# Accumulating transfers for three of the four sums of weights of a pair, and sums of h in steps

## The chip, the core and the metric

The kernel runs on one core of one Trainium2 chip. The metric is the time of one execution on the device in microseconds (us); for a kernel it is the median over its runs. The engines have their usual names: TensorE (PE, with its weight loads as PEld), VectorE (DVE), ScalarE (ACT), GpSimd (POOL) and SyncE (SP), which here only issues transfers.

## The reference, cut to what matters

The kernel computes one layer of a streaming encoder for one sequence of 512 tokens and width 2048, and a last RMSNorm. Everything is float32. An adaLN-modulated RMSNorm gives h, one wide projection of h gives the inputs of an mLSTM branch (4 heads of 256) and of a chunked attention branch (8 heads of 128) and two gates, and both branches come together in one output projection.

```python
h = rmsnorm(x, norm_g) * (1.0 + scale[:, None]) + shift[:, None]
proj = h @ w_in
(mq, mk, mv, mo, mz, mi, mf, aq, ak, av, az, g_m, g_a) = split_columns(proj)
y_m = mlstm_branch(mq, mk, mv, mo, mz, mi, mf, b_if, conv_w, conv_b, mh_norm_g)
y_a = chunk_attention_branch(aq, ak, av, az, rel_bias)
merged = jax.nn.sigmoid(g_m) * (y_m @ w_proj_m) + jax.nn.sigmoid(g_a) * (y_a @ w_proj_a)
return x + gate[:, None] * (merged @ w_out)        # and then rmsnorm(..., final_norm_g)
```

The change touches `h @ w_in`: how some of the columns of this projection are computed.

## The kernel before

**Products in two halves.** Float32 factors are split into a high and a low float16 part (`split`, lines 166 and 167: ScalarE writes `hi`, VectorE then writes `lo` from the source and `hi`), and TensorE makes three products out of them (hi*hi, hi*lo, lo*hi). Each group of weights gets a power of two as its scale: ScalarE squares each loaded half unit (`do_squares`, line 235), TensorE adds the sums up over the partitions (`do_tots`, through `tot_of`, line 150), and VectorE makes the scale and its inverse from the exponent (`scale_of`, lines 157 to 162).

**Units and jobs.** A unit is 128 columns (or 256 columns by half the depth) of a weight matrix, and is loaded as two transfers of 512 KB (128 partitions of 1024 float32). `jobs()` lists what is to be made, in order: single units (`u`, two chunks of 48 matmuls), tokens (`t`, two units, four chunks), projections (`p`) and pairs (`s`). A chunk is planned at 2.6 us in a pair and at 5.2 us in the others (`CHUNK_US`). A pair computes two units at once by Strassen's scheme in Winograd's form, with seven half-size products in place of eight: seven chunks of 24 matmuls. There are 32 pairs: 27 in which the two units belong to one group and share a scale (`same`), and five that pair a q with a k and have two scales (mixed).

**What a pair needs.** Its weights are four quarters: x11 and x21, the halves of the first unit, and x12 and x22, those of the second. Of them and of four sums seven weight tiles are made: 11, 22, t2, 21, t3, t1, t4, in that order (`of_pair`). The sums are made in place by VectorE: `p22` makes two of them after tile 22 is split, `p2` the third (line 273, or 275 in a mixed pair), `p21` the fourth (line 293). On the other side h is needed in its four quarters and four sums of quarters: `h_sums` makes them with four operations on 128x2048 elements (line 551) and four splits, all of them behind the first chunk of the first job. `strassen` (line 939 on) runs the seven products and adds them into the two results out of PSUM: ScalarE copies (lines 963, 964, 977), VectorE adds scaled results (line 947, and 986 for the fifth product).

**Buffers and order.** Loads go into a ring of eight buffers (`NST`); a load is issued when the oldest buffer's last reader is done (`can_load`, `free`). Weight tiles go into nine buffers (`NW`), so tiles are made up to nine ahead of their use. `stream(c)` stands behind every chunk and keeps everything going by a planned clock: loads (`do_dma`, on SP's queue), squares 7.0 us behind the load, totals 2.5 us behind the squares, scales, and then tiles (`make_after`). The order on TensorE at the beginning is written out by hand; elsewhere the framework sets the order on each engine when the kernel is built, and an engine then takes its instructions strictly in that order. The attention and the mLSTM heads run beside the jobs as generators (`side`, `advance`), and `heads` is started with the first job.

Of the kernel before, what the change touches and what calls it, by code (L numbers as in the profile page):

```python
# [9 lines left out]
F32 = mybir.dt.float32  # L10
# [33 lines left out]
def jobs():  # L44

    def s(kind, h, kind2=None):
        return ("s", (kind, h, 0), (kind2 or kind, h + (kind2 is None), 0))

    def u(kind, h, part=0):
        return ("u", (kind, h, part))

    def t(kind, h):
        return ("t", (kind, h, 0), (kind, h, 1))

    j = [u("k", 2), t("v", 0), t("v", 2), s("z", 2), s("q", 3, "k"), s("q", 4, "k"), t("v", 4), s("z", 4),
         s("q", 5, "k"), u("if", 0), s("q", 6, "k"), t("v", 6), s("z", 6), s("q", 7, "k")]
# [24 lines left out]
def block_kernel(ctx: ExitStack, tc: tile.TileContext, A, out):  # L83
# [98 lines left out]

    groups_w, group_of, loads = [], {}, []
    for j, job in enumerate(todo):
        i = first[j]
        if job[0] == "s":
            loads += [(i, 0), (i + 1, 1), (i + 1, 0), (i, 1)]
            gs = [[i, i + 1]] if job[1][0] == job[2][0] else [[i], [i + 1]]
# [26 lines left out]
    def width(x):  # L215
        return KT * 8 if x[0] == UIF else HW

    def do_dma(n=None):

        while at["dma"] < (len(loads) if n is None else n) and can_load() and not (n is None and at["other"]):  # L220
            x = loads[at["dma"]]
            st[x] = stage_tile(f"st_{x[0]}_{x[1]}")
            i, part = x
            src = A["w_if"] if i == UIF else A["w_u"][i - 1 if i > UIF else i][:, part * HW:(part + 1) * HW]
            nc.sync.dma_start(st[x]["tile"][:, 0:width(x)], src)
            when["dma", at["dma"]] = at["clock"]
            at["dma"] += 1

    def do_squares(n):
        while at["sq"] < min(n, at["dma"]):  # L230
# [3 lines left out]
            with nc.allow_low_precision(reason="only the exponent of the sum is used"):  # L234
                ACT.activation(junk(width(x)), st[x]["tile"][:, c], AF.Square, accum_out=ssq[x])  # L235
            when["sq", at["sq"]] = at["clock"]
            at["sq"] += 1

# [24 lines left out]
    def of_pair(j):  # L263
# [4 lines left out]

        def sub_or_mix(to, a, b, op, ratio):

            a, b, to = (st[x]["tile"] for x in (a, b, to))
            if same or ratio is None:
                V.tensor_tensor(to, a, b, op)  # L273
            else:
                V.scalar_tensor_tensor(to, b, ratio, a, ALU.mult, ALU.add)

        r = []

        def p22():
            tile_w("22", x22)  # L280
            if not same:
                r.append(times(scs[i][0], scs[i + 1][1], -1.0, f"r{i}"))
                r.append(times(scs[i + 1][0], scs[i][1], 1.0, f"n{i}"))
            sub_or_mix(x22, x22, x12, ALU.subtract, None)
            sub_or_mix(x12, x12, x11, ALU.subtract, r[0] if r else None)

        def p2():
            sub_or_mix(x11, x11, x22, ALU.add, r[1] if r else None)
            tile_w("t2", x11)

        def p21():
            tile_w("21", x21)
            V.tensor_tensor(st[x21]["tile"], st[x21]["tile"], st[x11]["tile"], ALU.subtract)
            st[x11]["free"] = True
# [57 lines left out]
    def stream(c):  # L352
# [5 lines left out]
        do_squares(n)  # L358
        do_tots(wait=2.5)
        do_scales()  # L360
# [185 lines left out]

    def h_sums():

        for to, a, b, op in (("22", "21", "22", ALU.add), ("21", "11", "21", ALU.subtract),
                             ("11", "22", "11", ALU.subtract), ("12", "12", "11", ALU.subtract)):  # L550
            V.tensor_tensor(of_h(to), of_h(a), of_h(b), op)
        for s, q in (("s4", "12"), ("s2", "11"), ("s3", "21"), ("s1", "22")):
            split(H[s][:, 0], H[s][:, 1], of_h(q), s_h)

# [344 lines left out]
    def finish(u, n):  # L899
# [35 lines left out]
        elif kind in ("ga", "gm"):  # L935
            ACT.activation(n, n, AF.Tanh, scale=0.5)
            th_g[kind, h] = n

    def strassen(j):

# [13 lines left out]
        def p1():  # L954
            go("a", (i, "11"), "11")
            for m, u in enumerate((u1, u2)):
                t, f = dest(u, i + m)
                n.append(t)
                if m and group_of[i] == group_of[i + 1]:
                    iw.append(iw[0])  # L960
                else:
                    iw.append(times(scs[i + m][1], i_h, f, f"u{i + m}"))
            ACT.activation(n[0][:, HT:S], ps["a"][:, 0:HT], AF.Copy, scale=iw[0])
# [144 lines left out]
    m_pool = None  # L1108
    side.append([heads(), P_])
    since = 0.0  # L1110
    for j in range(JO):
        if j == JG:
# [13 lines left out]
        for c, e in enumerate(CHUNKS[todo[j][0]](j)):  # L1126
# [170 lines left out]
```

## Time and profile before

| | before |
|---|---|
| median of three runs | 1645.82 us (1645.82, 1649.27, 1645.82) |
| the profiled execution | 1642.06 us, its span 1640.3 us |
| TensorE busy | 1515.1 us, 92% |
| VectorE busy | 1157.4 us, 71% |
| ScalarE busy | 959.6 us, 59% |
| GpSimd busy | 26.3 us, 2% |
| read from HBM, written | 204.91 MB, 4.19 MB |

The profile is of one execution; a busy share is an average over stages with different limits, so it only says where to look. Until about 157 us the scale, the shift and the first units of the projection are made from the large adaLN matrix. Then come the jobs: attention inputs to about 506 us, the mLSTM heads to about 956 us, the gates and projections to about 1460 us, and the output. A wait is put down to what released it last. Matmuls are pipelined, so a group's mean duration is longer than the distance at which its matmuls start; the distance is what counts.

### The profile page before, as it was taken

What the parts mean: (1) busy time and instruction counts of PE and PEld (TensorE: products, weight loads), DVE (VectorE), ACT (ScalarE), POOL (GpSimd) and SP (SyncE); (2) the same over time, 40 slices, a digit from 0 to 9 for tenths busy, and PEclk for the clock granted to TensorE, in tenths of its full rate; (3) what the DMA queues carried; (4) which work ended last, traced back from release to release, by engine and by line L of the source; (5) the groups of instructions that cost most, each with busy time, mean ns of one, the idle gap of its engine ahead of it and who ended that gap; (6) DMA issues with size and microseconds to landing.
All of it is one profiled execution on the core that took longest, in us unless ns stands there. A gap on an engine that the chain in (4) does not pass through costs nothing.

```text
span 1640.3 us, 29263 instructions
## 1 busy us (share of the span) xinstructions
PE 1515.1 (92%) x12087; PEld 1202.1 (73%) x12087; DVE 1157.4 (71%) x1901; ACT 959.6 (59%) x1504; POOL 26.3 (2%) x30
## 2 busy tenths in 40 slices
PE   1799699999999999999999999999999999999997
PEld 0345578787888888888888876766776776768887
DVE  7987968766676666576566597777789897664443
ACT  3225856666476385395484677655656766775522
POOL 4100000000000000000000000000000000000000
PEclk9999899999999999999999999999999999999999
DMA  9893223323141142152141233334456533373202
GB/s 388 344 393 116 82 83 98 95 94 107 55 160 54 52 141 66 52 168 65 52 155 52 78 105 126 117 103 155 129 193 203 168 119 129 117 226 108 91 2 103
DMA packets 59637, 210.99 MB, mean 129 GB/s; under 512 B 7520, under 2 KB 12272, under 8 KB 55024
## 3 DMA queue, kind: packets, MB, share of 16 engines
q1 hardware_dynamic: 59504, 209.13, 37.3%
q8 instruction: 94, 1.54, 0.4%
q14 instruction: 39, 0.32, 0.1%
HBM read 204.91 MB, written 4.19 MB: 127 GB/s over the span
## 4 chain that ended last, share of the span: by engine, by line
PE 40%; DVE 28%; ACT 14%; DMA 11%; issue 7%; SPq 0%; ACTq 0%; DVEq 0%
DMA st<-in_w_u 8%; DVE w L167 6%; PE pre L477 5%; ACT junk L235 4%; DVE st L273 4%; ACT w L166 4%; PE po L585 3%; PE po L587 3%; PE po L586 3%; DVE w_t L167 3%; PE ps L560 3%; PE ps L562 3%; PE ps L561 3%; PE ps L587 2%; PE ps L586 2%
## 5 line engine op out<-in xcount | busy, mean ns | idle before, releaser
L167 DVE SCALAR_TENSOR_TENSOR w<-st,sc_w,w 128x1024 f16<-128x1024 f32 x227 | 288.8, 1277 | 139.2 <-ACT w L166 129.2
L235 ACT ACTIVATE junk<-st 128x1024 uint8<-128x1024 f32 x259 | 272.0, 1050 | 132.0 <-DMA st<-in_w_u 125.3
L166 ACT ACTIVATE w<-st,sc_w 128x1024 f16<-128x1024 f32 x227 | 256.0, 1136 | 34.7 <-PE ps L562 16.5
L166 ACT ACTIVATE w_t<-st,sc_w 128x1024 f16<-128x1024 f32 x128 | 145.2, 1141 | 131.3 <-DVE st L273 60.1
L167 DVE SCALAR_TENSOR_TENSOR w_t<-st,sc_w,w_t 128x1024 f16<-128x1024 f32 x128 | 163.6, 1280 | 67.7 <-ACT w_t L166 66.7
L575 PE MATMUL psb<-hs,w_t 128*128 128x256 f16 x512 | 140.2, 274 | 9.1 <-DVE c L947 9.1
L561 PE MATMUL ps<-h,w 128*128 128x256 f16 x544 | 148.3, 273 | 0.3 <-DVE h L167 0.3
L560 PE MATMUL ps<-h,w 128*128 128x256 f16 x544 | 148.3, 273 | 0.0
L562 PE MATMUL ps<-h,w 128*128 128x256 f16 x544 | 148.3, 273 | 0.0
L586 PE MATMUL ps<-w,h 128*128 128x256 f16 x512 | 140.5, 275 | 6.2 <-DVE w L167 6.2
L585 PE MATMUL po<-w,m 128*128 128x256 f16 x512 | 140.1, 274 | 2.3 <-ACT m L166 2.3
L575 PE MATMUL psa<-h,w 128*128 128x256 f16 x512 | 141.2, 276 | 0.0
L576 PE MATMUL psa<-h,w 128*128 128x256 f16 x512 | 141.1, 276 | 0.0
L577 PE MATMUL psa<-h,w 128*128 128x256 f16 x512 | 141.0, 275 | 0.0
L587 PE MATMUL ps<-w,h 128*128 128x256 f16 x512 | 140.6, 275 | 0.0
L585 PE MATMUL ps<-w,h 128*128 128x256 f16 x512 | 140.4, 275 | 0.0
L577 PE MATMUL psb<-hs,w_t 128*128 128x256 f16 x512 | 140.3, 274 | 0.0
L576 PE MATMUL psb<-hs,w_t 128*128 128x256 f16 x512 | 140.2, 274 | 0.0
L586 PE MATMUL po<-w,m 128*128 128x256 f16 x512 | 139.8, 274 | 0.0
L587 PE MATMUL po<-w,m 128*128 128x256 f16 x512 | 139.6, 274 | 0.0
L576 PEld LDWEIGHTS <-w_t 128*128 128x128 f16 x1024 | 100.5, 98 | 32.4 <-issue 20.8
L477 PE MATMUL pre<-B,wpre 128*128 128x512 f32 x224 | 100.8, 606 | 12.0 <-ACT B L446 12.0
(267 smaller groups left out, 3411.9 us busy)
## 6 DMA issues: line engine op xcount, KB each, us to landing
st<-in_w_u SPq DMA_DIRECT2D x258, 512.0 KB, 4.3
ada<-in_w_ada SPq DMA_DIRECT2D x30, 1024.0 KB, 6.9
B<-in_w_adag SPq DMA_DIRECT2D x21, 512.0 KB, 5.9
wpre<-in_w_pre SPq DMA_DIRECT2D x16, 448.0 KB, 7.4
gst<-in_w_adag SPq DMA_DIRECT2D x11, 512.0 KB, 3.6
B<-in_xT SPq DMA_DIRECT2D x4, 1024.0 KB, 8.1
xo_s<-in_x SPq DMA_DIRECT2D x24, 128.0 KB, 4.8
out<-xo_s SPq DMA_DIRECT2D x12, 256.0 KB, 2.4
```

The costliest lines, as they stand in the source:

```text
L166: ACT.activation(hi, src, AF.Copy, scale=s_)
L167: V.scalar_tensor_tensor(lo, src, s_, hi, ALU.mult, ALU.subtract)
L235: ACT.activation(junk(width(x)), st[x]["tile"][:, c], AF.Square, accum_out=ssq[x])
L560: PE.matmul(ps, lhsT=hi, rhs=xhi(k), start=(n == 0), stop=False)
L561: PE.matmul(ps, lhsT=hi, rhs=xlo(k), start=False, stop=False)
L562: PE.matmul(ps, lhsT=lo, rhs=xhi(k), start=False, stop=(n == len(ks) - 1))
L575: PE.matmul(ps, lhsT=hi, rhs=x[:, 0, k, :], start=(k == 0 and not more), stop=False, **kw)
L576: PE.matmul(ps, lhsT=hi, rhs=x[:, 1, k, :], start=False, stop=False, **kw)
L577: PE.matmul(ps, lhsT=lo, rhs=x[:, 0, k, :], start=False, stop=(k == K2 - 1), **kw)
L585: PE.matmul(ps, lhsT=xq[:, 0, k % K2, ts], rhs=w[:, 0, c], start=(k == 0), stop=False)
L586: PE.matmul(ps, lhsT=xq[:, 0, k % K2, ts], rhs=w[:, 1, c], start=False, stop=False)
L587: PE.matmul(ps, lhsT=xq[:, 1, k % K2, ts], rhs=w[:, 0, c], start=False, stop=(k == KT - 1))
```

## The change

For each of the 27 pairs with one scale three of the four sums become transfers on GpSimd's queue that add into a buffer in SBUF (`add_in`). x12 gets x11 added from HBM behind its square; VectorE then makes one sum, x11 = x12 + x22; x22 gets x12's source added from HBM; and x21 gets that sum added from SBUF. Since such a transfer only adds, the scheme is turned into one with sums in place of differences: the second unit enters with its sign turned (`-f` in `strassen`, so that each unit of a pair now has its own factor), and the sums of h are changed to suit. A pair's loads come in the order x11, x12, x22, x21 instead of x11, x22, x12, x21. The mixed pairs keep four sums on VectorE.

The pair (q3, k3) is taken apart into two single units, which come right behind k2; that leaves 31 pairs, of which four are mixed. The sums of h become eight steps, of which two are made behind each chunk from the second on, and the heads start when four of them are done. Totals of squares come 5.0 us of planned time behind the squares instead of 2.5.

```diff
-    j = [u("k", 2), t("v", 0), t("v", 2), s("z", 2), s("q", 3, "k"), s("q", 4, "k"), t("v", 4), s("z", 4),
+    j = [u("k", 2), u("q", 3), u("k", 3), t("v", 0), t("v", 2), s("z", 2), s("q", 4, "k"), t("v", 4), s("z", 4),
...
-            loads += [(i, 0), (i + 1, 1), (i + 1, 0), (i, 1)]
+            loads += [(i, 0), (i + 1, 0), (i + 1, 1), (i, 1)]
+            if job[1][0] == job[2][0]:
+                gs, t1_of[i + 1, 0] = [[i, i + 1]], (i, 0)
...
+    def add_in(to, x):
+
+        nc.gpsimd.dma_start(st[to]["tile"], x, accum_op=ALU.add)
...
+            if x in t1_of:
+                add_in(x, source(t1_of[x]))
             at["sq"] += 1
...
         def p22():
             tile_w("22", x22)
+            if same:
+                V.tensor_tensor(a(), b(), c(), ALU.add)
+                add_in(x22, source(x12))
+                return
+            r.append(times(scs[i][0], scs[i + 1][1], 1.0, f"r{i}"))
+            r.append(times(scs[i + 1][0], scs[i][1], 1.0, f"n{i}"))
+            V.tensor_tensor(c(), c(), b(), ALU.add)
+            V.scalar_tensor_tensor(b(), a(), r[0], b(), ALU.mult, ALU.add)
+
+        def p2():
             if not same:
+                V.scalar_tensor_tensor(a(), c(), r[1], a(), ALU.mult, ALU.add)
             tile_w("t2", x11)
 
         def p21():
             tile_w("21", x21)
-            V.tensor_tensor(st[x21]["tile"], st[x21]["tile"], st[x11]["tile"], ALU.subtract)
+            if same:
+                add_in(x21, a())
+            else:
+                V.tensor_tensor(d(), d(), a(), ALU.add)
             st[x11]["free"] = True
...
-        do_tots(wait=2.5)
+        do_tots(wait=5.0)
...
+    s_neg = const.tile([P, 1], F32, name="s_neg")
+    V.tensor_scalar(s_neg, s_h, -1.0, None, ALU.mult)
+
+    def sums_of_h():
+
+        of = {q: of_h(q) for q in ("11", "12", "21", "22")}
+        return [lambda: V.tensor_tensor(of["22"], of["21"], of["22"], ALU.subtract),
+                lambda: V.tensor_tensor(of["21"], of["11"], of["21"], ALU.subtract),
+                lambda: V.tensor_tensor(of["11"], of["22"], of["11"], ALU.subtract),
+                lambda: V.scalar_tensor_tensor(of["12"], of["12"], -1.0, of["11"], ALU.mult, ALU.subtract),
+                lambda: split(H["s4"][:, 0], H["s4"][:, 1], of["12"], s_h),
+                lambda: split(H["s2"][:, 0], H["s2"][:, 1], of["11"], s_h),
+                lambda: split(H["s3"][:, 0], H["s3"][:, 1], of["21"], s_h),
+                lambda: split(H["s1"][:, 0], H["s1"][:, 1], of["22"], s_neg)]
...
-                if m and group_of[i] == group_of[i + 1]:
-                    iw.append(iw[0])
-                else:
-                    iw.append(times(scs[i + m][1], i_h, f, f"u{i + m}"))
+                iw.append(times(scs[i + m][1], i_h, -f if m else f, f"u{i + m}"))
...
             if j == 0 and c == 0:
-                h_sums()
                 for i in range(1, NPRE):
                     pre_out(i)
+            elif steps:
+                for f in steps[:2]:
+                    f()
+                steps = steps[2:]
+                if len(steps) == 4:
+                    side.append([heads(), P_])
```

## Rows read from the trace of the kernel before

**Rows 1.** The page's first part: busy us, share of the span, instructions.

```profile
PE 1515.1 (92%) x12087; PEld 1202.1 (73%) x12087; DVE 1157.4 (71%) x1901; ACT 959.6 (59%) x1504; POOL 26.3 (2%) x30
```

**Rows 2.** Busy time by stretch; columns PE, PEld, DVE, ACT, POOL, clock, DMA share, GB/s.

```profile
156.00:193.00 37.00, 22.84 (x164) 17.22 (x163) 36.26 (x38) 30.81 (x38) 0.00 (x0) 0.82 0.14 45
...
956.00:1460.00 504.00, 480.89 (x3630) 350.85 (x3628) 396.27 (x584) 332.32 (x482) 0.00 (x0) 0.99 0.45 148
```

**Rows 3.** Waits of PE, 156 to 200 us: total us, times, longest us.

```profile
PE tot_w L150 <- ACT junk L235: 7.3, 4, 2.8
PE ps L586 <- DVE w L167: 6.2, 2, 3.9
```

**Rows 4.** Waits of PE, 200 us to the end.

```profile
PE psb L575 <- DVE c L947: 16.9, 20, 3.5
PE tot_w L150 <- ACT junk L235: 12.9, 14, 2.2
```

**Rows 5.** Timeline of PE, 171 to 190 us: start us, duration us, instruction.

```profile
173.38 0.27 PE L586 MATMUL ps<-w,h 128*128 128x256 f16 x1 [2.27 <-DVE w L167]
173.49 0.27 PE L587 MATMUL ps<-w,h 128*128 128x256 f16 x1
...
188.41 0.42 PE L585 MATMUL ps<-w,h 128*128 128x256 f16 x1
188.62 0.42 PE L586 MATMUL ps<-w,h 128*128 128x256 f16 x1
```

**Rows 6.** Timeline of DVE, 167 to 190 us.

```profile
167.04 2.28 DVE L551 TENSOR_TENSOR B<-B 128x2048 f32<-128x2048 f32 x1
...
179.91 6.87 DVE L167 SCALAR_TENSOR_TENSOR hs<-B,sc_h,hs 128x2048 f16<-128x2048 f32 x3
186.70 3.67 DVE L167 SCALAR_TENSOR_TENSOR w<-st,sc_w,w 128x1024 f16<-128x1024 f32 x3
```

**Rows 7.** Timeline of DVE in the gate stage, 1062 to 1084 us.

```profile
1067.18 1.22 DVE L273 TENSOR_TENSOR st<-st,st 128x1024 f32<-128x1024 f32 x1
1068.31 0.47 DVE L947 SCALAR_TENSOR_TENSOR c<-psb,tm_u,c 128x256 f32<-128x256 f32 x1
...
1069.95 1.23 DVE L273 TENSOR_TENSOR st<-st,st 128x1024 f32<-128x1024 f32 x1
```

**Rows 8.** Groups by form on DVE: count, busy us, mean ns, idle before.

```profile
L167 DVE SCALAR_TENSOR_TENSOR w_t<-st,sc_w,w_t 128x1024 f16<-128x1024 f32 x128 | 163.6, 1280 | 67.7 <-ACT w_t L166 66.7
L273 DVE TENSOR_TENSOR st<-st,st 128x1024 f32<-128x1024 f32 x86 | 104.9, 1220 | 0.9
L293 DVE TENSOR_TENSOR st<-st,st 128x1024 f32<-128x1024 f32 x32 | 39.0, 1219 | 0.3
...
L142 DVE TENSOR_SCALAR tm_u<-inv_w,inv_h 128x1 f32<-128x1 f32 x71 | 14.0, 210 | 1.3
```

**Rows 9.** Busy time of one stretch behind a wait, columns as in Rows 2.

```profile
1070.00:1075.00 5.00, 5.00 (x34) 3.89 (x33) 3.20 (x7) 3.94 (x5) 0.00 (x0) 0.68 0.01 4
```

**Rows 10.** Loads into the ring (tile st), 956 to 1460 us.

```profile
DMA to landing us min/median/max: 3.4/4.6/6.3
```

**Rows 11.** DMA issues: count, KB each, median us to landing.

```profile
st<-in_w_u SPq DMA_DIRECT2D x258, 512.0 KB, 4.3
ada<-in_w_ada SPq DMA_DIRECT2D x30, 1024.0 KB, 6.9
```

**Rows 12.** Timeline of ACT in the gate stage, 1062 to 1084 us.

```profile
1074.19 1.14 ACT L166 ACTIVATE w_t<-st,sc_w 128x1024 f16<-128x1024 f32 x1
...
1078.61 1.15 ACT L166 ACTIVATE w_t<-st,sc_w 128x1024 f16<-128x1024 f32 x1 [1.52 <-PE psb L577]
```

**Rows 13.** Waits of SP's queue: total us, times, longest us.

```profile
SPq L225 <- DVE st L293: 303.9, 29, 23.7
```

**Rows 14.** Line 468, divided over DVE and POOL: duration ns min/median/max, first and last start.

```profile
L468 DVE TENSOR_TENSOR B<-B,rstd x2: 1744/1748/1751, 28.2 to 29.9; 128x512 f32<-128x512 f32 x2
```

**Rows 15.** Line 420, a sum of the same size: duration ns min/median/max.

```profile
L420 DVE TENSOR_TENSOR gac<-gac,B x4: 685/689/692, 1155.6 to 1335.1; 128x512 f32<-128x512 f32 x4
```

More of the change, by code (lines that the diff above doesn't have):

```diff
@@ L180, in block_kernel @@
     UIF = units.index(("if", 0, 0))
-    groups_w, group_of, loads = [], {}, []
+    groups_w, group_of, loads, t1_of = [], {}, [], {}
     for j, job in enumerate(todo):
@@ L186, in block_kernel @@
         if job[0] == "s":
-            loads += [(i, 0), (i + 1, 1), (i + 1, 0), (i, 1)]
-            gs = [[i, i + 1]] if job[1][0] == job[2][0] else [[i], [i + 1]]
+            loads += [(i, 0), (i + 1, 0), (i + 1, 1), (i, 1)]
+            if job[1][0] == job[2][0]:
+                gs, t1_of[i + 1, 0] = [[i, i + 1]], (i, 0)
+            else:
+                gs = [[i], [i + 1]]
         else:
@@ L216, in width, with source @@
         return KT * 8 if x[0] == UIF else HW
+    def source(x):
+        i, part = x
+        return A["w_if"] if i == UIF else A["w_u"][i - 1 if i > UIF else i][:, part * HW:(part + 1) * HW]
+    def add_in(to, x):
+        nc.gpsimd.dma_start(st[to]["tile"], x, accum_op=ALU.add)
     def do_dma(n=None):
@@ L222, in do_dma @@
             st[x] = stage_tile(f"st_{x[0]}_{x[1]}")
-            i, part = x
-            src = A["w_if"] if i == UIF else A["w_u"][i - 1 if i > UIF else i][:, part * HW:(part + 1) * HW]
-            nc.sync.dma_start(st[x]["tile"][:, 0:width(x)], src)
+            nc.sync.dma_start(st[x]["tile"][:, 0:width(x)], source(x))
             when["dma", at["dma"]] = at["clock"]
@@ L267, in of_pair @@
         same = group_of[i] == group_of[i + 1]
[L269 to L273, printed above, removed]
-            else:
-                V.scalar_tensor_tensor(to, b, ratio, a, ALU.mult, ALU.add)
+        a, b, c, d = ((lambda x=x: st[x]["tile"]) for x in (x11, x12, x22, x21))
         r = []
@@ L280, in p22 @@
             tile_w("22", x22)
-            if not same:
[L282 to L288, printed above, removed]
+            if same:
[7 more added lines that the diff above has]
+        def p2():
+            if not same:
+                V.scalar_tensor_tensor(a(), c(), r[1], a(), ALU.mult, ALU.add)
             tile_w("t2", x11)
@@ L292, in p21 @@
             tile_w("21", x21)
-            V.tensor_tensor(st[x21]["tile"], st[x21]["tile"], st[x11]["tile"], ALU.subtract)
+            if same:
+                add_in(x21, a())
+            else:
+                V.tensor_tensor(d(), d(), a(), ALU.add)
             st[x11]["free"] = True
@@ L545, in block_kernel @@
             split(H[q][:, 0, c, :], H[q][:, 1, c, :], of_h(q)[:, c, :], s_h)
[L547 to L553, printed above, removed]
+    s_neg = const.tile([P, 1], F32, name="s_neg")
[10 more added lines that the diff above has]
+                lambda: split(H["s1"][:, 0], H["s1"][:, 1], of["22"], s_neg)]
     def feat_mm(ps, wk, xhi, xlo, ks):
@@ L958, in p1 @@
                 n.append(t)
-                if m and group_of[i] == group_of[i + 1]:
-                    iw.append(iw[0])
-                else:
-                    iw.append(times(scs[i + m][1], i_h, f, f"u{i + m}"))
+                iw.append(times(scs[i + m][1], i_h, -f if m else f, f"u{i + m}"))
             ACT.activation(n[0][:, HT:S], ps["a"][:, 0:HT], AF.Copy, scale=iw[0])
@@ L1108, in block_kernel @@
     m_pool = None
-    side.append([heads(), P_])
     since = 0.0
+    steps = sums_of_h()
     for j in range(JO):
```

## The prediction

> **What bounds the kernel now.** I read the page's first part before anything else: TensorE is busy for 92% of the span and VectorE for 71% [rows 1]. So an edit that takes work from VectorE is worth only what TensorE waits for VectorE, and the second view is therefore the busy time by stages. Between 156 and 193 us TensorE is busy for 22.84 of 37 us, at a mean granted clock of 0.82; in the gate stage (956 to 1460 us) it is busy for 480.89 of 504 us while VectorE has 396 us of work [rows 2]. The loss is dense at the start and thin afterwards. Third, TensorE's waits. From 156 to 200 us it waits 7.3 us for squares of weights on ScalarE and 6.2 us for weight tiles that VectorE splits [rows 3]. After 200 us its two largest waits are 16.9 us for VectorE's evacuations of PSUM (20 times) and 12.9 us for squares (14 times) [rows 4]; no wait for a split weight tile is among them. Fourth, the timelines. In the first stretch VectorE works through the sums of h and their splits, from 167.04 to 186.78 us, and only then splits the three weight tiles that TensorE resumes with at 188.03 us [rows 5, 6]. In the gate stage the second sum of a pair stands right behind an evacuation on VectorE, and three sums and that evacuation fill 1067.18 to 1071.18 us [rows 7].
>
> **The start.** The sums of h are four operations of 2.28 us and four splits of 2.34 us, some 18.5 us of VectorE in one block. The change deals them out two at a time from the second chunk on, and puts two single units (q3, k3) ahead of the first tokens unit. A unit is 96 matmuls that start 0.11 us apart [rows 5], about 10.4 us; so units k2, q3 and k3 keep TensorE busy for 31 us, and they need two weight tiles each, which can be split directly behind the first evacuations. The first pair, which needs the sums, is two tokens units later still. What hides the moved 18.5 us is these 31 us of single units, in which VectorE has only four tiles of q3 and k3 (5 us) and the four of v0 (5 us): 28.5 us of work. That nearly fills the cover, so I keep 3 us of new waiting for v0's tiles, with ends 0 and 6. Removed are the waits of 7.3 + 6.2 = 13.5 us [rows 3], and the slow clock behind them: at 188.41 us matmuls start 0.21 us apart instead of 0.11 [rows 5], the lower of the two levels (1.2 GHz), for at most the 5 us to the end of that stretch, so at most 2.5 us lost; I take 2.3. Added: q3 and k3 cost 192 matmuls instead of a pair's seven products of 24, so 24 more at 0.11 = 2.6 us. Sum: -13.5 - 2.3 + 2.6 + 3 = **-10.2 us** (ends -13 and -7). The attention's first step starts two chunks (10 us) later; its waits later on are for other things, so I price that at nothing, and at 2 us if the cover of its 300 us is gone.
>
> **The sums of weights.** VectorE makes 86 sums at one place and 32 at another, 1.22 us each [rows 8]; 86 = 3 x 27 + 5, so 27 pairs have one scale and five are mixed. Of the four sums of each of the 27 three go: 81 x 1.22 = 98.8 us. Each such pair now needs its own factor for the second unit: 27 x 0.21 = 5.7 us back [rows 8]. VectorE's net relief is 93 us, beside other work: TensorE's waits show only 16.9 us of it. Half of these waits I expect to go, since weight splits and other evacuations stay in the queue: **-8.5 us** (ends 0 and -16.9). One such wait, at 1065 us, is followed by 5 us at a mean clock of 0.68 [rows 9], 1.6 us lost; with that one gone, **-1.6 us**. The totals of the squares are sent to TensorE 5 instead of 2.5 us of planned time behind the squares. In single units and tokens a chunk is planned at 5.2 us, so both come to the next chunk there; only in pairs (2.6 us) does it move. Of 12.9 us I take a quarter: **-3 us** (ends 0 and -8).
>
> **The transfers.** 81 transfers of 512 KB go on the POOL queue; POOL itself is busy for 26.3 us of the span [rows 1]. What is queued behind a waiting one there is the next transfer: the one of the next pair waits for a square on ScalarE, so it can hold back one of this pair. No row of this kernel is an accumulating transfer. The nearest: a plain load of 512 KB takes 4.3 us from issue to landing over the whole span, and 3.4 at least, 6.3 at most in the gate stage; one of 1024 KB takes 6.9 us [rows 10, 11]. An accumulating transfer moves its source and also reads what it adds to, so the 1024 KB row is nearest in bytes: I take **6.9 us**, with ends 3.4 (as fast as the fastest load) and 10.3 (6.9 behind another load of 3.4).
> The Trainium skill (page "DMA: Bandwidth & Descriptors", section "Anatomy of one DMA — SWDGE (gpsimd) path") fits 2.0 us plus bytes over 436 GB/s for a plain transfer from this queue; an estimate from it is 3.2 us, close to the low end, and no run here shows it.
> How long may one take? At 1068.40 us the pair's first sum is done. Its third tile is begun on ScalarE at 1074.19, 5.8 us later; its last at 1078.61 [rows 7, 12]. After the change that third tile waits for a transfer issued at the end of the one remaining sum: 5.8 us is break-even. The last tile waits for a transfer issued some 3.6 us behind the sum (two tiles of 1.14 us on ScalarE, one split of 1.28 us on VectorE [rows 8, 12]): 10.2 - 3.6 = 6.6 us. Mean: 6.2 us. Also, SP's loads have waited 304 us for the sum that releases the pair's first buffer, in 29 instances [rows 13]; now that buffer is released when the last transfer has landed, at the same break-even. Waiting behind such a tile are ScalarE's squares and VectorE's evacuations. What passes to TensorE: of 98.8 us of sums, 16.9 appeared as waits, 0.17. At 6.9 us: 27 x 0.7 x 0.17 = 3.2, **+4 us** with the swapped load order. At 3.4 us: 27 x -2.8 x 0.17 = -13 us. At 10.3 us the delay exceeds what a chunk (2.6 us) can hide and I let half pass (between 0.17 and 1): 27 x 4.1 x 0.5 = +55 us. In the gate stage, 16 such pairs add 48 x 0.52 = 25 MB to 148 GB/s x 504 us = 75 MB, so a DMA share of 0.45 becomes some 0.6 [rows 2]: room on the average.
>
> **Sum.** -10.2 - 8.5 - 1.6 - 3 + 4 = -19.3 us. The profiled execution took 1642.06 us (span 1640.3); it would take 1623. The median of the runs is 1645.82, so **1626.5 us** there, 1.2% less.
>
> **Rivals.** First, *late transfers*: the transfers take longer than the lead hides, ScalarE sits before the third and last tile of each pair, and evacuations and totals behind it are late. It decides from the point where 27 x (L - 6.2) x 0.5 eats the 24 us gained elsewhere: L = 8.0 us. At 9 us it is 27 x 2.8 x 0.5 = 38, so about 1660; at 10.3 us 1677. For it speaks that ScalarE already waits for the sums of weights, and that loads take up to 6.3 us in just that stage; against it that no wait of TensorE after 200 us is for a weight tile. Second, *sums that were hidden anyway*: only the start gains, the evacuations are late behind splits rather than sums: -10.2 + 4, so 1640. Third, *VectorE pays for POOL*. At the start the two work at once: VectorE's sum of 128x512 takes 1748 ns beside those that the same line gives to POOL, and 689 alone [rows 14, 15]. If making each transfer's descriptors holds VectorE for that 1.06 us, 81 of them give 86 of the 93 us back, and a transfer that waits for a split in turn (1.28 us) takes 8.2 us: -10.2 - 3 + 27 x 2.0 x 0.17 = -4, so 1642, at the bound of what can be told. Against it: the row is of two sums at once, not of descriptors, so its chance is small. The Trainium skill (page "SBUF — State Buffer", section "SBUF: two separate sides") states this mechanism: some VectorE operations keep POOL from writing descriptors, so that the DMA engines starve. It names operations in a two-port mode, and no run here shows whether the splits are of that kind. That the change does not do what it says I see no room for: the third sum of each pair is the only one left for VectorE.
>
> **Chances.** About 0.2% (3.3 us) can be told from no change. Forecast (a gain of 8 to 37 us): 0.50. Hidden sums (1636 to 1642): 0.14. VectorE pays for POOL, or gain and loss cancel: 0.12. Late transfers: 0.24, most of it below 1677. So faster 0.64, same 0.12, slower 0.24. The range reaches from all gains with transfers of 3.4 us, 1645.8 - 23.3 - 13 = 1609, to 1677: about 0.08 is left out below and 0.08 above.
>
> **What would show it.** Right: no TensorE gap over 2 us from 168 to 193 us and no low clock there; VectorE's busy time lower by some 90 us; accumulating transfers landing in 5 to 8 us; waits for evacuations near 8 us. Wrong: ScalarE waiting for transfers before third and last tiles by over 2 us each, with waits of TensorE behind them (late transfers); splits over 1.28 us or sums over 1.22 us (VectorE pays for POOL); a wait of over 6 us at the first tokens unit (the start's cover is too short).

## The result and the profile after

The changed kernel takes 1658.8 us (median of 7 runs, 1653.65 to 1661.7) against 1645.82 us before: a ratio of 1.0077, 95% interval 1.0053 to 1.0101. It is slower by 0.8%, where 1.2% faster was forecast. The profiled execution has a span of 1653.6 us.

The page's first part, its queues (packets, MB, share of 16 engines) and its issues (KB each, us to landing):

```profile
PE 1527.0 (92%) x12111; PEld 1209.2 (73%) x12111; DVE 1057.1 (64%) x1834; ACT 955.5 (58%) x1500; POOL 96.8 (6%) x111
...
q0 software_dynamic: 11664, 42.47, 14.2%
...
st<-in_w_u POOLq DMA_DIRECT2D x54, 512.0 KB, 5.5
st<-st POOLq DMA_DIRECT2D x27, 512.0 KB, 5.0
```

VectorE has 100 us less to do than in [rows 1] (89 of them by the sums: with these back on VectorE, in e2 below, it is busy for 1146.2 us), and the kernel is slower nevertheless. The 81 transfers are there, and their medians to landing are 5.0 and 5.5 us, sooner than the 6.9 us that the prediction took. So neither the work removed nor the transfer's length was misjudged in the direction that would explain the loss. Where it lies, the stretches show (columns as in [rows 2]):

```profile
156.00:193.00 37.00, 35.72 (x309) 29.68 (x308) 36.59 (x45) 36.94 (x44) 0.00 (x0) 1.00 0.31 103
956.00:1470.00 514.00, 473.60 (x3478) 342.08 (x3476) 333.04 (x524) 315.87 (x453) 38.10 (x44) 0.96 0.65 183
```

The start has become dense: TensorE is busy for 35.72 of the 37 us, at full clock, where [rows 2] has 22.84 at 0.82. In the gate stage it is the other way round: 473.60 busy in 514 us at 0.96, where [rows 2] has 480.89 in 504 at 0.99. I split both traces at the same matmuls (first of tile kq, last of ph, first of po). Before, the stages take 383.3 us from 156.6 us to the heads, 392.4 for the heads, 529.4 for the gate stage and 178.5 behind it. After, they take 368.1, 383.2, **566.6** and 179.1. So the start gains 15 us, the heads 9, and the gate stage loses 37: TensorE's gaps there grow from 22.9 to 45.5 us, and the time at the lower clock (1.2 GHz) from 10.2 to 44.4 us, which costs half of itself (matmuls 0.21 instead of 0.11 us apart, as in [rows 5]).

Waits of PE from 200 us to the end, to set beside [rows 4]:

```profile
PE psb L593 <- DVE c L967: 20.8, 11, 5.1
PE tot_w L150 <- ACT junk L244: 15.7, 7, 5.0
PE tot_w L150 <- DVE u_w L157: 7.7, 8, 4.4
```

The first two are fewer but longer: the longest was 3.5 us and is 5.1. What is ahead of them on VectorE and ScalarE, in the gate stage (930 to 1475 us):

```profile
DVE w_t L167 <- ACT w_t L166: 69.0, 37, 5.4
DVE w L167 <- ACT w L166: 39.3, 22, 6.0
```

The same view of ScalarE:

```profile
ACT w_t L166 <- DMA st<-in_w_u: 60.0, 16, 7.3
ACT w_t L166 <- DMA st<-st: 14.2, 7, 3.0
```

VectorE stands for 69.0 + 39.3 = 108.3 us before low halves whose high halves ScalarE has not made. In the trace of before the same two waits sum to 50.3 us in that window:

```profile
DVE w L167 <- ACT w L166: 37.1, 22, 4.8
DVE w_t L167 <- ACT w_t L166: 13.2, 14, 1.4
```

The difference, 58 us, is as much as VectorE saved there in sums: 16 pairs x 3 x 1.22 [rows 8]. ScalarE in turn stands 74 us before the tiles that are changed by transfers. Before, it stood 47 us for the sums that VectorE made for such tiles:

```profile
ACT w_t L166 <- DVE st L273: 30.9, 14, 3.8
ACT w_t L166 <- DVE st L293: 15.8, 9, 2.7
```

One pair shows it (timelines: start, duration, and in brackets the idle time before and what ended it). POOL and VectorE, from 1224 us:

```profile
1224.74 0.88 POOL L227 DMA_DIRECT2D st<-in_w_u  x1 [25.03 <-ACT junk L244]
1224.80 1.22 DVE L286 TENSOR_TENSOR st<-st,st 128x1024 f32<-128x1024 f32 x1
...
1226.32 0.86 POOL L227 DMA_DIRECT2D st<-in_w_u  x1 [0.70 <-DVE u_w L157]
```

ScalarE, tile 21 and the first tile behind it:

```profile
1227.11 1.13 ACT L166 ACTIVATE w<-st,sc_w 128x1024 f16<-128x1024 f32 x1
1235.23 2.19 ACT L166 ACTIVATE w_t<-st,sc_w 128x1024 f16<-128x1024 f32 x2 [6.99 <-DMA st<-in_w_u]
```

VectorE, behind tile t3:

```profile
1236.41 1.28 DVE L167 SCALAR_TENSOR_TENSOR w_t<-st,sc_w,w_t 128x1024 f16<-128x1024 f32 x1 [5.43 <-ACT w_t L166]
1237.61 0.74 DVE L1003 SCALAR_TENSOR_TENSOR c<-psc,tm_u,c 128x512 f32<-128x512 f32 x1
```

ScalarE and TensorE, the next long wait for squares:

```profile
1246.16 0.63 ACT L1096 ACTIVATE junk<-m 128x512 uint8<-128x512 f32 x1 [3.81 <-DVE m L1095]
...
1246.92 1.06 ACT L244 ACTIVATE junk<-st 128x1024 uint8<-128x1024 f32 x1
...
1248.12 0.16 PE L150 MATMUL tot_w<-ssq,onesb 128*128 128x1 bf16 x1 [4.34 <-ACT junk L244]
```

The pair's one sum ends at 1226.02. At 1224.74 POOL has issued t1's transfer of the next pair, at 1226.32 it issues t3's of this one. The first of the two lands after 5.2 us, t3's after 8.8. (Two loads that SP issued from 1226.77 on were in flight too.) Tile t3 starts at 1235.23, 9.2 us behind the sum; ScalarE has stood for 6.99 us, and VectorE behind it for 5.43, with an evacuation (L1003) queued behind. At 1248.12 a wait of TensorE for squares ends, of 4.34 us. The square before it (1246.92) has no idle time in front: it stood in line behind line 1096, for which ScalarE had waited 3.81 us on VectorE. So it is in the whole stage: of the 15 us that TensorE waits there for squares, all but 0.3 us are for squares with no idle time of ScalarE in front, so none of these stood waiting for its own load. Behind the wait TensorE runs at half clock (1248 to 1253 us; columns as in [rows 2]):

```profile
1248.00:1253.00 5.00, 3.86 (x20) 2.75 (x20) 3.46 (x9) 4.13 (x8) 0.00 (x0) 0.50 0.42 128
```

### The profile page after: what moved, and what is told of

It is laid out like the page before. It is cut to its first block, busy times and chain, and to the rows that moved or that the text cites. A ratio compares the mean times of both kernels' runs of the same rounds, so it can differ in the third digit from the quotient of the medians.

```text
span 1653.6 us, 29576 instructions
## 1 busy us (share of the span) xinstructions
PE 1527.0 (92%) x12111; PEld 1209.2 (73%) x12111; DVE 1057.1 (64%) x1834; ACT 955.5 (58%) x1500; POOL 96.8 (6%) x111
## 3 DMA queue, kind: packets, MB, share of 16 engines
q0 software_dynamic: 11664, 42.47, 14.2%
## 4 chain that ended last, share of the span: by engine, by line
PE 39%; DMA 18%; issue 17%; DVE 15%; ACT 10%; POOL 1%; SPq 0%; ACTq 0%; POOLq 0%; DVEq 0%
DMA st<-in_w_u 12%; PE pre L488 5%; DVE w L167 4%; PE po L603 3%; PE po L605 3%; PE po L604 3%; PE ps L578 3%; PE ps L580 3%; PE ps L579 3%; ACT junk L244 3%; DMA st<-st 3%; ACT w L166 3%; PE ps L605 2%; PE ps L604 2%; PE ps L603 2%
## 5 line engine op out<-in xcount | busy, mean ns | idle before, releaser
L167 DVE SCALAR_TENSOR_TENSOR w_t<-st,sc_w,w_t 128x1024 f16<-128x1024 f32 x124 | 158.5, 1281 | 184.5 <-ACT w_t L166 165.9
L166 ACT ACTIVATE w_t<-st,sc_w 128x1024 f16<-128x1024 f32 x124 | 140.7, 1143 | 157.2 <-DMA st<-in_w_u 63.6
L579 PE MATMUL ps<-h,w 128*128 128x256 f16 x608 | 166.2, 273 | 0.2 <-DVE h L167 0.2
L578 PE MATMUL ps<-h,w 128*128 128x256 f16 x608 | 166.4, 274 | 0.0
L580 PE MATMUL ps<-h,w 128*128 128x256 f16 x608 | 166.1, 273 | 0.0
L593 PE MATMUL psb<-hs,w_t 128*128 128x256 f16 x496 | 140.1, 283 | 23.0 <-DVE c L967 20.1
L593 PE MATMUL psa<-h,w 128*128 128x256 f16 x496 | 138.8, 280 | 3.4 <-ACT c L981 3.4
L594 PE MATMUL psa<-h,w 128*128 128x256 f16 x496 | 138.9, 280 | 0.0
L595 PE MATMUL psa<-h,w 128*128 128x256 f16 x496 | 138.7, 280 | 0.0
L594 PEld LDWEIGHTS <-w_t 128*128 128x128 f16 x992 | 99.0, 100 | 40.1 <-issue 27.6
L227 POOL DMA_DIRECT2D st<-in_w_u x54 | 46.8, 883 | 1175.8 <-ACT junk L244 372.3
```

The lines of the kernel that those rows point to most:

```text
L166: ACT.activation(hi, src, AF.Copy, scale=s_)
L167: V.scalar_tensor_tensor(lo, src, s_, hi, ALU.mult, ALU.subtract)
L578: PE.matmul(ps, lhsT=hi, rhs=xhi(k), start=(n == 0), stop=False)
L579: PE.matmul(ps, lhsT=hi, rhs=xlo(k), start=False, stop=False)
L580: PE.matmul(ps, lhsT=lo, rhs=xhi(k), start=False, stop=(n == len(ks) - 1))
L593: PE.matmul(ps, lhsT=hi, rhs=x[:, 0, k, :], start=(k == 0 and not more), stop=False, **kw)
```

## The experiments

The table has all runs: the ratio to before (95% interval), and from each profiled execution the length of the gate stage, VectorE's waits before low halves in it, and the mean time from the start of a pair's first tile (11) on ScalarE to the end of its last low half (t4) over the 16 pairs of the gate stage. Each ratio is to the kernel before on the same chip; its median there was 1642.84 to 1646.15 us, so a difference of a few us between medians of two rows says nothing.

| kernel | ratio | gate stage, us | VectorE waits, us | t4 ready, us |
|---|---|---|---|---|
| before | 1 | 529.4 | 50.3 | 19.1 |
| after | 1.0077 (1.0053, 1.0101) | 566.6 | 108.3 | 19.7 |
| e1 gate pairs' sums on VectorE | 0.9831 (0.9814, 0.9847) | 527.0 | 34.9 | 18.6 |
| e2 all sums on VectorE | 0.9812 (0.9791, 0.9833) | 522.8 | 40.1 | 18.5 |
| e3 before, with the start alone | 0.9851 (0.983, 0.9872) | 523.1 | 43.6 | 19.0 |
| e4 totals at 2.5 | 1.0179 (1.0162, 1.0196) | 579.1 | 127.0 | 20.1 |
| e5 t4 alone by transfer | 1.0032 (1.0016, 1.0048) | 558.4 | 85.9 | 21.4 |
| e6 t3 alone | 0.9831 (0.9811, 0.9851) | 535.8 | 58.4 | 18.8 |
| e8 t1 alone | 0.9839 (0.982, 0.9857) | 524.2 | 31.2 | 16.6 |
| e11 t1 and t3 | 0.9943 (0.9922, 0.9964) | 548.8 | 85.6 | 19.5 |
| e7 plain transfers | 0.9827 (0.98, 0.9855) | 532.0 | 70.7 | 17.6 |
| e9 t4, other source | 1.0049 (1.003, 1.0067) | 559.6 | 103.4 | 22.2 |
| e10 first buffer held | 0.9885 (0.9853, 0.9918) | 537.1 | 35.3 | 18.5 |
| e12 nine staging buffers | 1.0151 (1.0127, 1.0175) | 566.1 | 121.9 | 21.0 |
| e13 no transfer, held at t4 | 0.9837 (0.9807, 0.9866) | 530.2 | 50.9 | 19.0 |
| e16 t1 alone, held at t4 | 0.9815 (0.9783, 0.9847) | 520.3 | 34.5 | 16.9 |
| e14 tile t1 before t3 | 1.0032 (1.0012, 1.0052) | 564.0 | 111.2 | 19.8 |
| e15 t4's transfer earlier | 0.999 (0.997, 1.0011) | 545.0 | 70.0 | 18.5 |
| e17 t4 alone, planned later | 1.0032 (1.0014, 1.005) | 560.4 | 91.5 | 21.1 |
| e18 all, planned later | 1.0015 (0.9996, 1.0034) | 554.3 | 109.0 | 19.7 |

### Which part loses: e1, e2, e3, e4

e1 and e2 are the changed kernel with sums made by VectorE, in the gate pairs alone and in all 27:

```diff
-            if same:
+            if same and todo[j][1][0] not in ("ga", "gm"):     # e2: if False
                 V.tensor_tensor(a(), b(), c(), ALU.add)
                 add_in(x22, source(x12))
                 return
+            if same:
+                V.tensor_tensor(c(), c(), b(), ALU.add)
+                V.tensor_tensor(b(), b(), a(), ALU.add)
+                return
```

(p2 then makes `a + c`, p21 `d + a`, both on VectorE; t1's transfer is not issued.)

> The changed kernel with the sums of the 16 gate pairs made by VectorE again; the 11 other pairs keep their transfers. In the profiles the changed kernel is 18 us ahead at the first key-query product of the mLSTM and 25 us ahead at the last transposes of its heads, and 13 us behind at the first output product: it loses 38 us between, in the gate stage. Theory of late transfers: the gate stage takes about as long as in the kernel before (531 us from the last head's transposes to the first output product, against 569 in the changed kernel), so some 25 us less than before, ratio 0.985. Rival, the planned order (totals at 5.0 us, order of loads): these stay in, so the loss in the gate stage stays, ratio about 1.007.

> The changed kernel with all sums of weights on VectorE, no transfer on POOL's queue; the start, the order of loads and the totals at 5.0 us stay. Late transfers: the gate stage is as in the run with VectorE's sums in the gate stage alone; if the 33 transfers of the other stages helped, this one is slower than that by the part of the 25 us that is theirs (up to 10 us), if they are worth nothing both agree within 3 us. Planned order: ratio about 1.007 here too.

e3 is the kernel before with q3 and k3 as single units and the sums of h in steps; e4 is the changed kernel with one number undone:

```diff
-        do_tots(wait=5.0)
+        do_tots(wait=2.5)
```

> The kernel before with the change's start alone: q3 and k3 as single units behind k2, and the sums of h two at a time; sums of weights, order of loads and totals as before. The prediction put the start at -10 us; the traces show 18 us at the first key-query product. If the start makes these 18 us, ratio 0.989; if 8 of them are the transfers' in the attention stage, 0.994.

> The changed kernel with totals of squares at 2.5 us of planned time behind the squares, as before. Late transfers: the loss in the gate stage stays (ratio 1.005 to 1.012), since the squares themselves are late. Planned order: the scales come earlier and the loss goes (ratio below 1.0).

Without any transfer the kernel takes 1612.08 us, 47 us less than with them and 34 less than before; no version is faster (e16, at 1611.53, is the same). The transfers of the gate stage carry nearly all of it (e1: 1616.85). The start alone gives 1619.84, a gain of 26 us. e4 is worse than the changed kernel by 15 us: the later totals are no cause of the loss, they lessen it.

### Which transfer: e5, e6, e8, e11

One sum by transfer each, the others on VectorE; e11 is the changed kernel with `V.tensor_tensor(d(), d(), a(), ALU.add)` in place of t4's transfer. In e8 x12 holds t1 already when VectorE starts on the sums, so it makes t2 as x22 + x12 in x22's place and t3 as t2 - x11 in x11's.

> The changed kernel with one transfer a pair: x21 += t2 (the last tile's sum, SBUF to SBUF); the other three sums on VectorE. All sums on VectorE gave 0.981 of before, all three transfers 1.0077: 44 us between. Theory of standing in line (ScalarE and VectorE wait at a tile whose transfer is late, and evacuations and squares stand behind): this transfer has two tiles between issue and use and costs little, 0 to 10 us, ratio 0.981 to 0.987. Theory of late buffers (the pair's first buffer is released only when this transfer has read it, so the next loads, squares and totals are late): this one carries most of the loss, 20 to 40 us, ratio 0.993 to 1.005.

> The changed kernel with one transfer a pair: x22 += x12 from HBM (the third tile's sum, issued behind the sum t2); the other three on VectorE. Standing in line: in the changed kernel ScalarE sat idle for 3 to 7 us before this tile in the gate stage; this one carries most of the 44 us, ratio 0.993 to 1.005. Late buffers: ratio 0.981 to 0.987.

> The changed kernel with one transfer a pair: x12 += x11 from HBM (the sum t1), issued behind the square and so long before the tiles; VectorE then makes t2 = x22 + t1 in x22's place, t3 = t2 - x11 in x11's, and t4: three sums of four. Both theories: no tile waits for it, so no loss against all sums on VectorE (0.981) and up to 5 us gained by the 33 us less of VectorE, ratio 0.978 to 0.982. If any transfer on POOL's queue disturbs (VectorE held by descriptors, DMA engines shared), it is a third of the 44 us slower, ratio 0.990.

> The changed kernel with t4's sum back on VectorE; t1 and t3 by transfers. The converse of the run with t4's transfer alone. If the parts add up (t3's 4 us, t1's 4 us, t4's 36), ratio 0.983 to 0.988. If any two transfers together fill the queue, ratio over 0.995.

By the medians, and against e2, t4 alone costs 36 us, t3 alone 4, t1 alone 4 (both inside the noise), t1 and t3 together 23, all three 47 (44 by the ratios). That t4's carries most is what the account of late buffers had said, and t3's what the account of standing in line had. The traffic as such is not the cause: the 27 transfers of e8 take 5.0% of the DMA engines' span, those of e5 5.2%. Waits of ACT in the gate stage of e5:

```profile
ACT w_t L166 <- DMA st<-st: 55.4, 16, 5.3
...
ACT w_t L166 <- DVE st L296: 38.8, 15, 5.9
```

The same of e6:

```profile
ACT w_t L166 <- DMA st<-in_w_u: 44.6, 14, 5.1
...
ACT w_t L166 <- DVE st L287: 13.5, 8, 2.5
```

ScalarE waits some 3 us per pair for the transfer in both. But t3's transfer also takes a sum away ahead of tile t2 (38.8 becomes 13.5), so the pair's last tile is ready after 18.8 us instead of 18.5. t4's transfer takes none away there: 21.4 us. A likely reason why t1 and t3 cost more together than 4 + 4 is in the issues: in e11 12 of 29 transfers of the gate stage are issued less than 4 us behind the one before (11 of them 0.5 to 2.1 us), a t1's and a t3's side by side, as at 1224.74 and 1226.32 above; in e6 none is. The slowest in e11 lands after 9.1 us, in e6 after 7.1. (Late ones occur without that: in e8, where they are issued 14 us apart or more in this stage, one landed after 9.6 us while SP's queue moved 2.2 MB.)

### Adding or moving: e7

```diff
-        nc.gpsimd.dma_start(st[to]["tile"], x, accum_op=ALU.add)
+        nc.gpsimd.dma_start(st[to]["tile"], x)
```

> The changed kernel with plain copies in place of the 81 accumulating transfers, same queue, sizes and waits; the sums are left out, so the output is not the reference's. If adding costs time in the transfer (the destination is read too), landing falls from 5.5 us towards the 4.2 of a load and much of the 44 us goes, ratio 0.985 to 0.998. If it is the queue and the transfer as such, landing stays at 5 us or more and the time within 0.3% of the changed kernel, ratio 1.005 to 1.010.

Every engine has the same instructions in the same order as in the changed kernel (but for two neighbours on VectorE, lines 689 and 910), and the same bytes are issued. The page of e7 (queue, issues):

```profile
q0 software_dynamic: 11664, 42.47, 7.3%
...
st<-in_w_u POOLq DMA_DIRECT2D x54, 512.0 KB, 4.1
st<-st POOLq DMA_DIRECT2D x27, 512.0 KB, 3.2
```

The queue's time on the DMA engines is 7.3% instead of 14.2%, landing 1.4 and 1.8 us shorter, and the kernel 44 us faster. In the gate stage tile t4 starts 14.8 instead of 16.8 us behind the pair's first tile, and the mean distance from one pair to the next is 30.93 instead of 32.99 us: 2.0 us earlier, 2.06 us less. This is the cleanest pair of all: in that order, the time that adding costs in the transfers is worth the 44 us, and the pairs come later by as much as their last tiles do. It does not say by which way: with the tiles the buffers come free later too, and the DMA engines are busier.

### Where the lateness acts: e9, e10, e12, e13, e16

My first account was late buffers: t4's transfer holds x11, so that SP's loads come late. e9 adds another source (an HBM block, so x11 is not held, and tile t4 still waits); e10 is e2 with a store of x11 that holds it and delays no tile; e12 is the changed kernel with `NST, NW = 9, 8` in place of 8 and 9.

```diff
-                add_in(x21, a())
+                add_in(x21, source(x11))
```

```diff
             if same:
+                V.tensor_scalar(a()[:, 0:1], a()[:, 0:1], 1.0, None, ALU.mult)
+                nc.gpsimd.dma_start(scratch, a())
```

> As the run with the last tile's transfer alone (1.0032 of before, 36 us over all sums on VectorE), but the transfer adds a block from HBM in place of t2, so that it doesn't hold the pair's first buffer; what it adds is not the sum, so the output is not the reference's. The tile t4 still waits for it. Late buffers: the loss goes, ratio 0.981 to 0.988. Standing in line at t4: it stays, ratio 0.998 to 1.006.

> All sums on VectorE (0.981 of before), and behind the sum of the last tile one plain transfer on POOL's queue that stores t2 to a block in HBM that nothing reads: the pair's first buffer is held until it has been read, but no tile waits. Late buffers: this alone brings 20 to 36 us, ratio 0.993 to 1.003. Standing in line: ratio 0.981 to 0.985.

> The changed kernel with nine load buffers and eight weight tiles in place of eight and nine (both do not fit with one more). Late buffers: a buffer more takes up the late release, and at least half of the 44 us goes, ratio 0.981 to 0.996. Standing in line: tiles are made one fewer ahead, so the waits at them show more, ratio 1.005 to 1.03.

e9 loses as e5 does (1652.13 against 1648.52), e10 loses 13 us against e2, and a ninth buffer at the cost of a weight tile makes it worse (which tests both at once). As the whole of the loss the account fell; the held buffer is a smaller part.

The second account was that ScalarE stands in line at t4, with squares behind. e13 (e2) and e16 (e8) have three thrown-away squares in front of t4:

```diff
         def p(key, x, held=False):
+            if held:
+                for w_ in (HW, HW, HT):
+                    ACT.activation(junk(w_), st[x]["tile"][:, 0:w_], AF.Square)
             tile_w(key, x)
```

> The kernel with all sums on VectorE (no transfer at all), with three more ScalarE operations in front of tile t4 of each of the 27 pairs: squares of 1024, 1024 and 512 elements, thrown away, 1.05 + 1.05 + 0.6 = 2.7 us. That is what ScalarE stands still more at t4 when t4 is a transfer (55.4 against 14.3 us in 16 pairs of the gate stage). Standing in line is the whole of it: it is as bad as t4's transfer alone, gate stage near 560 us, ratio 1.00 to 1.005. The transfers themselves (their traffic, the buffer) do the harm: ScalarE is only 59% busy and takes the 2.7 us, gate stage near 526, ratio 0.981 to 0.985.

> Only t1 by transfer (ratio 0.984, ScalarE stands 12 us before pair tiles in the gate stage), with the same three thrown-away squares in front of t4 as in the run with all sums on VectorE. If the total counts and some 55 us are free: 12 + 16 x 2.7 = 55, nearly no loss, gate stage 525 to 532, ratio 0.984 to 0.989. If it is the place that counts (whatever stands in line at t4): the same loss as there, some 30 to 40 us, ratio 1.002 to 1.008.

The third square has 256 elements, not 512: 1.05 + 1.05 + 0.40 = 2.5 us by e13's trace. e13 costs 4 us against e2, inside the noise, e16 nothing against e8. So ScalarE has room for the squares. But the run tests less than I wrote: tile t4 starts only 0.9 us later than in e2 (16.2 against 15.3 us behind tile 11), where e5's starts 3.6 us later (18.9). The order that was made at build time is another one in e13, on ScalarE and on VectorE, and it has these squares in it. VectorE's waits in the gate stage, of e5:

```profile
DVE w_t L167 <- ACT w_t L166: 53.5, 25, 4.2
DVE w L167 <- ACT w L166: 32.4, 26, 3.4
```

The same of e13:

```profile
DVE w L167 <- ACT w L166: 33.4, 30, 3.0
...
DVE w_t L167 <- ACT w_t L166: 17.5, 17, 2.3
```

### Can the place be mended: e14, e15, e17, e18

e14 makes tile t1 ahead of t3 in the changed kernel; e15 is e5 with tile 21 ahead of t2, so that t4's transfer is issued one tile earlier; e17 is e5, and e18 the changed kernel, with thrown-away squares on ScalarE in front of the tiles that wait.

```diff
-        return [lambda: tile_w("11", x11), p22, p2, p21, lambda: p("t3", x22), lambda: p("t1", x12),
+        return [lambda: tile_w("11", x11), p22, p2, p21, *((t1, t3) if same else (t3, t1)), ...   # e14
+        return [lambda: tile_w("11", x11), *((p22, p21, p2) if same else (p22, p2, p21)), ...     # e15
```

```diff
+            for w_ in hold if same else ():                    # e17: t4 (HW, HW, HT); e18: t3 (HW,) * 3, t4 (HW,)
+                ACT.activation(junk(w_), W[ready][:, 0, 0:w_], AF.Square)
             tile_w(key, x)
```

> The changed kernel with tile t1 made ahead of t3 in the 27 pairs, so t3's transfer has one tile more (1.14 us on ScalarE, 1.28 us on VectorE) before ScalarE needs it. If the total of ScalarE's standing before pair tiles counts: 60 us at t3 in the gate stage fall by some 16 x 1.2 = 19, 85 become 66 in all, as with t1 and t3 by transfer, gate stage near 546, ratio 0.992 to 0.997. If the transfers hurt in another way, or the wait only moves on to t4: as the changed kernel, 1.005 to 1.010.

> Only t4 by transfer, as in the run with 1.0032, but tile 21 is made ahead of t2 behind the three sums: ScalarE makes 21 while VectorE makes the sums that t2 needs, and the transfer for t4 is issued one tile earlier. If ScalarE's standing counts: 38.8 us at t2 fall to some 20 and 55.4 at t4 to some 36, 94 become 56 in all, gate stage 526 to 535, ratio 0.981 to 0.987. If the transfer hurts by its traffic or by the buffer that it holds: unchanged, 1.000 to 1.005.

> Only t4 by transfer, as in the run with 1.0032, with three thrown-away squares (2.7 us, of a tile that is long ready) in front of t4 on ScalarE: they fill the time in which ScalarE stood there, so tile t4 starts on the chip about when it did, but the order that is set at build time now knows that it comes late and can put evacuations ahead of its low half on VectorE. Account A (an order made without the transfer's length: VectorE stands 85.9 us in the gate stage before low halves, against 40 to 51 without transfers, and what is queued behind it is late): these waits fall to some 50, gate stage 528 to 538, ratio 0.983 to 0.990. Account B (the transfer, or the late buffer behind t4, whatever the order): gate stage 558 to 570, ratio 1.003 to 1.010.

> The changed kernel with the same filling: three squares of 1024 (3.15 us) in front of t3, where ScalarE stands 60 us in 16 pairs, and one (1.05 us) in front of t4, where it stands 14. Account A: VectorE's waits before low halves fall from 108 us in the gate stage to some 60, gate stage 532 to 548, ratio 0.987 to 0.996, faster with 112 us more of work on ScalarE. Account B: gate stage 567 or more, ratio 1.007 to 1.015.

Only e17 comes out as one account had it (B, the transfer whatever the order: gate stage 558 to 570, and 560.4 measured); the others fall between or beside. In e14 the wait moves on from t3 to t4 (ScalarE stands 25.3 us for the one and 38.8 for the other, 60.0 and 14.2 in the changed kernel). e15 brings the last tile back to 18.5 us and gains 6 us on e5 by the median, not 30; its squares wait 74.1 us for loads in the gate stage, where e2's wait 52.1. In e17 tile t4 is begun at 18.4 us instead of 18.9, so the lateness remains, and with it the loss: an order that knows of the delay does not help by itself. e18 does gain 12 us in the gate stage, but in the profiled executions gives 10 back in the stage ahead of the heads (377.7 instead of 368.1 us).

## Why the prediction was wrong

**The start** was right in its mechanism and too small. Waits of PE from 156 to 200 us after the change:

```profile
PE tot_w L150 <- ACT junk L244: 0.8, 2, 0.6
```

Of the two waits of [rows 3] one has fallen from 7.3 to 0.8 us and the other is gone, the low clock (0.82) as well, and the 3 us of new waiting for v0's tiles did not come. Predicted -10.2 us, measured 15 less in that stage, and 26 in all for the start alone (e3): the heads and the gate stage gain as well, which the sum did not have. The heads that start two chunks later cost nothing.

**VectorE's sums** failed. Of the -8.5 us nothing is seen. e7 has 87 us less of VectorE's work than e2 (1059.0 against 1146.2 us busy) and no adding transfer, and at 1614.81 us it is not faster than e2 at 1612.08. TensorE's waits for evacuations from 200 us on, in e7:

```profile
PE psb L593 <- DVE c L967: 16.9, 12, 3.8
```

That is the figure of [rows 4]. e7 still has tiles that wait for its transfers; e8 has next to none (28 us less of VectorE's work than e2, the least standing before low halves), and waits 15.4 us for evacuations, e2 14.9. The rival of sums that were hidden anyway is right on this point. The -1.6 us for one low-clock stretch became 17 us of loss in low-clock time (44.4 against 10.2 us, by half).

**The totals** at 5.0 are worth -15 us beside late transfers (e4), not -3. What they are worth without these was not tried.

**The transfers** are the step that turned the sign: they and the sums that they replace were to bring -4.5 us (+4 and -8.5), and cost 47 by the medians and 44 by the ratios (after against e2). Their length was not the error: I took 6.9 us to landing, and they land after 5.0 to 5.5, in the gate stage after 5.6 to 6.0. By the prediction's own formula that would have been a gain. Both other factors were wrong. The break-even of 6.2 us read [rows 7, 12] as if the 5.8 us from the first sum to the third tile were all slack. But that time holds the two other sums; with them gone, tile t2 is ready 3.7 us sooner (8.1 against 11.8 us behind tile 11) and only tile 21 is queued ahead of t3, so ScalarE and VectorE stand there. In the pair above ScalarE is done with tile 21 at 1228.24, 2.2 us behind the sum, where the prediction had 5.8. And the share that passes, 0.17, came from work that VectorE does at any free time. A late tile in an in-order queue is no such work: from e7 to the changed kernel the last tile starts 2.0 us later and the pairs are 2.06 us further apart, and against e2 a last tile that is ready 0.6, 2.6, 2.9 and 3.8 us later (e13, e17, e5, e9) goes with pairs that are 0.5, 2.4, 2.3 and 2.4 us further apart. So most of the delay passes, up to some 2.4 us. 16 x 2.06 = 33 us come out of lengths that the prediction held to be harmless.

**The rivals.** Late transfers, which had 0.24, is what happened: ScalarE before third and last tiles, evacuations and totals late behind them, all as described. Only its point of decision was wrong: it was to need 8.0 us to landing and decided below 6. That its 1660 us for transfers of 9 us lies beside the 1658.8 measured is chance. That VectorE pays for POOL did not happen: beside 81 transfers the splits take 1281 ns and the sums 1219 (lines of after):

```profile
L167 DVE SCALAR_TENSOR_TENSOR w_t<-st,sc_w,w_t 128x1024 f16<-128x1024 f32 x124 | 158.5, 1281 | 184.5 <-ACT w_t L166 165.9 <-PE psd L595 17.8
...
L286 DVE TENSOR_TENSOR st<-st,st 128x1024 f32<-128x1024 f32 x27 | 32.9, 1219 | 0.2 <-DMA st<-in_w_u 0.2
```

against 1280 and 1220 in [rows 8]; the idle time in front of them is what grew, from 67.7 to 184.5 us. The rule of the Trainium skill that was weighed there (page "SBUF — State Buffer", section "SBUF: two separate sides") has a transfer wait for VectorE rather than VectorE for POOL. It is not seen at work here either: of the adding transfers of e8 that ran without a packet on SP's queue, one landed after 5.3 us while VectorE was busy for 24% of that time, and twelve after 5.3 to 5.9 us while it was busy for 95% or more.

**What stays open.** Over all twenty kernels the gate stage grows by about half a microsecond for each microsecond that VectorE stands before low halves (correlation 0.95). That is a connection, not a cause that was isolated. Three places don't fit one law. Before, t4 is ready after 19.1 us and the pairs follow each other at 30.89 us, while 19.5 in e11 goes with 32.10, and 19.7 in the changed kernel with 32.99. e10 loses with less standing than e2. And e15 has its last tile in time and still loses 22 us in the gate stage, with loads that come late. Late tiles and late buffers (e10) both contribute; how they share the loss of the full change was not separated. Nor was the order: it is set anew at build time, and e5, e9 and e13 differ from e2 in it on TensorE, VectorE and ScalarE; only e7 against the changed kernel holds it fixed.

## What to carry over

Before a sum is moved from a busy engine to a transfer, ask what is queued in order behind its first reader: what no other work covers of the time from issue to landing enters that queue, and here nearly all of that reached TensorE, while the sum that was replaced had cost next to nothing. A break-even read from the trace of before must leave out the time that the removed work itself filled. And a change with two independent parts should be priced and tried as two: here the start alone gains 1.5% and the whole change without transfers 1.9%, and the transfers take back more than that.

## What the runs showed of the hardware

- An accumulating transfer of 512 KB costs the DMA engines twice what a plain one of the same bytes does: 14.2% against 7.3% of 16 engines' span for the same 42.47 MB (after, e7), and lands 1.4 us (from HBM) or 1.8 us (from SBUF) later. The source matters less: 5.5 us from HBM, 5.0 from SBUF. The plain one from HBM landed in 4.1 us. The plain one from SBUF landed in 3.2 us, which is what the Trainium skill's fit (page "DMA: Bandwidth & Descriptors", section "Anatomy of one DMA — SWDGE (gpsimd) path") gave as an estimate in the prediction; the adding one is outside that fit.
- POOL is busy for 0.88 us per adding issue and 0.53 us per plain one.
- An adding transfer lands later when others are in flight. Two of the changed kernel's, issued at 1124.90 and 1125.51 us with no load under way until 1132.92, landed after 5.4 and 7.7 us; two issued 1.6 us apart, at 1360.40 and 1362.03, after 5.4 and 6.3. Loads on SP's queue do it too: in e8, where thirteen adding transfers without such loads landed after 5.3 to 5.9 us, the one issued at 1214.9, beside 2.2 MB of loads, landed after 9.6.
